# Seven half-size products for the mixer's v with u, its gates and its output, gates and branches token-major, second half of the tokens reversed

## The chip, the cores and the metric

The kernel runs on one core of one Trainium2 chip. The metric is the device time of one execution in microseconds; lower is better. Work is split over TensorE (PE; its weight loads are shown as PEld), VectorE (DVE), ScalarE (ACT), GpSimd (POOL) and SyncE (SP). SP issues most DMAs, POOL those that accumulate and some others.

## The reference

Two layers, each of three residual steps, then a last RMSNorm; 512 tokens, 1024 channels, float32:

```python
for l in range(DEPTH):
    x = x + 0.5 * swiglu(rms_norm(x, ffn1_norm[l]), ffn1_w_in[l], ffn1_w_out[l])
    x = x + mixer(rms_norm(x, mix_norm[l]), ...)
    x = x + 0.5 * swiglu(rms_norm(x, ffn2_norm[l]), ffn2_w_in[l], ffn2_w_out[l])
return rms_norm(x, final_norm)

def mixer(h, ...):
    z = h @ w_in                      # q, k, v, u: 512 columns each; ga, gf: 1024 each
    y_na = neighbourhood_attention(q, k, v, rpb) @ w_na_out
    y_f = fourier_mix(u) @ w_f_out    # real part of a 2-D DFT over tokens and 128 channels
    return (sigmoid(ga + b0) * y_na + sigmoid(gf + b1) * y_f) @ w_o
```

The feed-forward part has 2816 hidden columns.

## The kernel before

**Arithmetic.** Each float32 operand is split into a high part in the matmul's own format (ACT, L277) and a low part, the difference (DVE, L278). `mm3` (L270) makes three matmuls of each product: high x high, high x low, low x high, 512 columns each.

**Weights.** A `Stream` (L235) walks a fixed list of items, each a 128 x 1024 piece. A piece is loaded by SP up to eight items ahead; `prep` (L165) splits it into `whi` and `wlo`, two items ahead of use, in three buffers each. In the mixer a raw piece takes a slot of the pool that activations use (23 slots of 4 KB a partition); in the feed-forward stages it has nine buffers of its own, in the space where the mixer keeps its bias, mask and temporary tiles. `swap_pools` (L995) goes from one to the other, and loads of the next stage begin there.

**Feed-forward stages.** `stage_ffn` (L410) works token-major: tokens stand on the output's partitions, and activations are the operand loaded into the array. The 1024 x 1024 by 1024 x 1024 products are done with seven products of half size (Strassen's scheme): products numbered 1 to 7, taken in the order 1, 5, 6, 2, 7, 3, 4, each of 24 matmuls (`product`, L390). Products 5, 6, 7 and 4 take sums or differences of activation quarters (t1, t2, t3, t4: `combo`, L456), made once a stage behind 96 plain matmuls. Weight sums come partly from accumulating DMAs on POOL (L154), partly from DVE additions (L171). `snap` (L510) copies a partial sum from PSUM, `less` (L516) subtracts it later.

**Norm.** `Norm.quad` (L337) transposes a quarter of x to channel-major by PE and splits it. `rstd` (L362) makes the scale of each token by some 13 tiny DVE operations. For the mixer, each 256-wide piece is split straight from PSUM (L281 on DVE).

**Mixer.** `stage_mixer` (L651) runs, a layer: `proj_U` (L697) with a mirrored copy of the second half of the tokens, since the token DFT takes sums and differences of token t and its mirror; `proj_V` (L741); the token transform `four_pos` (L758) on u's sums and differences; projections of q and k channel-major, 24 matmuls each; the channel transform `four_ch` (L776); eight attention blocks in a three-deep pipeline `att_step` (L894: scores, then transposes of the softmax, then the product with v); and for each of eight groups of 128 output channels two gates of 24 matmuls, the Fourier branch and the attention branch of 12 each, channel-major, where the token scale is spread over partitions as `R` (L382). The gates' biases are one value per partition, taken by ACT's tanh. Attention steps 6 to 9 stand between the first gates and branches. Last, the output product of 192 matmuls adds into x token-major (L978).

Each engine takes its instructions in a fixed order that the build decides; a wait holds all that stands behind it on that engine. POOL and SP issue their DMAs in such an order too.

## Time and profile before

| what | value |
|---|---|
| median of 3 runs | 1978.1 us (1977.86 to 1979.02) |
| the profiled execution | 1976.79 us |
| its span | 1975.0 us |
| mean granted clock of TensorE | 0.995 |
| HBM read, written | 321.43 MB, 2.10 MB |

The span runs from the first to the last instruction of the execution; the rest of its time lies around it. A row of the profile gives a line of the code, the engine, what is written from what, the count, busy time and mean nanoseconds of one, then the idle time of that engine just before, with what ended it. Matmuls overlap, so a matmul's own duration is longer than the step from one start to the next. Rows of stretches give span, busy time and instruction count of each engine, the granted clock of TensorE, the share of the DMA engines and GB/s.

### The profile page before, as it was taken

What the parts mean: (1) busy time and instruction counts of PE and PEld (TensorE: products, weight loads), DVE (VectorE), ACT (ScalarE), POOL (GpSimd) and SP (SyncE); (2) the same over time, 40 slices, a digit from 0 to 9 for tenths busy, and PEclk for the clock granted to TensorE, in tenths of its full rate; (3) what the DMA queues carried; (4) which work ended last, traced back from release to release, by engine and by line L of the source; (5) the groups of instructions that cost most, each with busy time, mean ns of one, the idle gap of its engine ahead of it and who ended that gap; (6) DMA issues with size and microseconds to landing.
All of it is one profiled execution on the core that took longest, in us unless ns stands there. A gap on an engine that the chain in (4) does not pass through costs nothing.

```text
span 1975.0 us, 24363 instructions
## 1 busy us (share of the span) xinstructions
PE 1942.8 (98%) x9077; PEld 1608.9 (81%) x9077; DVE 1516.8 (77%) x1835; ACT 1056.6 (54%) x1520; POOL 156.6 (8%) x194
## 2 busy tenths in 40 slices
PE   8999999999999999999999999999999999999997
PEld 6888887888888888888788888878888888888885
DVE  7677899598444777889977878996874447787897
ACT  7555666445333655566555556653553336555663
POOL 0011011200000000101000100102100000000010
PEclk9999999999999999999999999999999999999998
DMA  9577599232423367749757765974123234776692
GB/s 300 162 189 202 157 246 326 75 89 65 137 75 119 86 180 195 198 147 263 226 142 205 187 171 172 283 251 113 60 80 123 96 97 105 213 176 168 178 289 103
DMA packets 96630, 328.27 MB, mean 166 GB/s; under 512 B 11136, under 2 KB 13312, under 8 KB 96512
## 3 DMA queue, kind: packets, MB, share of 16 engines
q1 hardware_dynamic: 76416, 258.55, 38.6%
q0 software_dynamic: 20096, 68.17, 19.0%
q8 instruction: 71, 1.16, 0.2%
q14 instruction: 47, 0.39, 0.1%
HBM read 321.43 MB, written 2.10 MB: 164 GB/s over the span
## 4 chain that ended last, share of the span: by engine, by line
PE 87%; DVE 9%; issue 2%; ACT 2%; DMA 1%; SPq 0%; DVEq 0%; ACTq 0%
PE A L271 7%; PE A L272 7%; PE A L273 7%; PE ps L272 7%; PE ps L271 7%; PE ps L273 7%; PE o L272 5%; PE o L273 5%; PE o L271 5%; PE B L272 4%; PE B L271 4%; PE B L273 4%; DVE wlo L278 2%; PE tr L426 2%; PE C L272 2%; PE C L273 2%
## 5 line engine op out<-in xcount | busy, mean ns | idle before, releaser
L278 DVE TENSOR_TENSOR wlo<-raw,whi 128x1024 fp32r<-128x1024 f32 (+1 forms) x498 | 597.6, 1206 | 314.8 <-ACT whi L277 313.9
L277 ACT ACTIVATE whi<-raw 128x1024 fp32r<-128x1024 f32 (+1 forms) x498 | 515.1, 1037 | 534.0 <-PE A L273 122.0
L154 POOL DMA_DIRECT2D raw<-in_wst_dram x128 | 110.5, 873 | 1515.3 <-DMA raw<-in_wst_dram 1188.5
L171 DVE TENSOR_TENSOR raw<-raw,raw 128x1024 f32<-128x1024 f32 (+1 forms) x128 | 151.1, 1190 | 2.4
L271 PE MATMUL ps<-xh,whi 128*128 128x512 f32 x384 | 151.4, 394 | 0.0
L272 PE MATMUL ps<-xl,whi 128*128 128x512 f32 x384 | 149.8, 390 | 0.0
L273 PE MATMUL ps<-xh,wlo 128*128 128x512 f32 x384 | 149.7, 390 | 0.0
L273 PE MATMUL A<-whi,xl 128*128 128x512 f32 x320 | 124.7, 390 | 0.0
L271 PE MATMUL A<-whi,xh 128*128 128x512 f32 x320 | 124.6, 389 | 0.0
L272 PE MATMUL A<-wlo,xh 128*128 128x512 f32 x320 | 124.6, 389 | 0.0
L173 ACT ACTIVATE whi<-raw 128x1024 fp32r<-128x1024 f32 x64 | 66.2, 1035 | 60.0 <-PE B L273 33.2
L271 PEld LDWEIGHTS ps<-xh,whi 128*128 128x128 f32 x384 | 72.1, 188 | 16.4
L273 PEld LDWEIGHTS ps<-xh,wlo 128*128 128x128 f32 x384 | 72.1, 188 | 15.1
L272 PEld LDWEIGHTS ps<-xl,whi 128*128 128x128 f32 x384 | 72.2, 188 | 14.4
L174 DVE SCALAR_TENSOR_TENSOR wlo<-raw,whi 128x1024 fp32r<-128x1024 f32 x64 | 75.3, 1189 | 10.8 <-ACT whi L173 10.8
L271 PEld LDWEIGHTS A<-whi,xh 128*128 128x128 f32 x320 | 60.1, 188 | 12.4
L272 PEld LDWEIGHTS A<-wlo,xh 128*128 128x128 f32 x320 | 60.1, 188 | 12.4
L273 PEld LDWEIGHTS A<-whi,xl 128*128 128x128 f32 x320 | 60.1, 188 | 12.4
L513 ACT ACTIVATE sn<-A 128x512 f32<-128x512 f32 x80 | 47.8, 599 | 41.2 <-PE A L273 41.2
L271 PE MATMUL A<-whi,t2h 128*128 128x512 f32 x160 | 63.0, 394 | 3.2 <-ACT sn L513 3.2
L271 PE MATMUL B<-whi,t1h 128*128 128x512 f32 x160 | 64.1, 402 | 1.1 <-ACT whi L277 1.1
L272 PE MATMUL B<-wlo,t1h 128*128 128x512 f32 x160 | 63.2, 395 | 0.5 <-DVE wlo L278 0.5
(257 smaller groups left out, 4804.4 us busy)
## 6 DMA issues: line engine op xcount, KB each, us to landing
raw<-in_wst_dram SPq DMA_DIRECT2D x450, 512.0 KB
raw<-in_wst_dram POOLq DMA_DIRECT2D x120, 512.0 KB, 8.1
raw<-in_wst_dram SPq DMA_DIRECT2D x32, 256.0 KB
vs<-v SPq DMA_DIRECT2D x12, 256.0 KB
bw<-in_rpb_dram SPq DMA_DIRECT2D x32, 68.0 KB
xt<-in_xtr_dram SPq DMA_DIRECT2D x8, 256.0 KB
x<-in_xin_dram SPq DMA_DIRECT2D x4, 512.0 KB
raw<-in_wst_dram POOLq DMA_DIRECT2D x8, 256.0 KB, 8.2
```

The costliest lines, as they stand in the source:

```text
L154: G.dma_start(out=self.t, in_=wst[GRAN_AT[self.plus]][:, 0 : self.n], accum_op=ALU.add)
L171: V.tensor_tensor(t, t, self.add.t, ALU.add)
L173: S.activation(hi, t, AF.Copy, scale=-1.0)
L174: V.scalar_tensor_tensor(lo, t, -1.0, hi.bitcast(F32), ALU.mult, ALU.subtract)
L271: PE.matmul(ps, lh, rh, start=start, stop=False, skip_group_check=again)
L272: PE.matmul(ps, lh, rl, start=False, stop=False, skip_group_check=again)
L273: PE.matmul(ps, ll, rh, start=False, stop=stop, skip_group_check=again)
L277: S.activation(hi, src, AF.Copy)
L278: V.tensor_tensor(lo, src, hi.bitcast(F32), ALU.subtract)
L426: PE.transpose(tr[:, k, b * P : (b + 1) * P], a[:, b, (q + k) * P : (q + k + 1) * P], ident)
L513: S.activation(t[:, b, :], ps[b], AF.Copy)
```

## The change

The mixer's three large products go over to the seven-product scheme of the feed-forward stages, with the functions `product`, `snap`, `less`, `combo` moved out so that both use them:

- v and u together are one 1024-column product; the gates are two blocks (first and second 512 columns of both gates); the output product is one. Weight pieces of a layer rise from 48 to 72 items (7 x 2 for each of four products, 8 for q and k, 4 each for the branches), with four accumulating DMAs a product.
- The norm keeps the mixer's raw quarters and splits them 1024 wide. t1, t2, t3 and t4 are made in the first product block, written to DRAM (`park`) and read back for the gates (`unpark`), all by POOL's queue.
- The second half of the tokens stands in reverse order in the mixer's activations, so that no mirrored copy is needed; q, k, y and the attention output are turned back, or written turned, in their own copies. v's second half is mirrored by four matmuls with a flipped identity. The shifted copies of v are now issued by POOL.
- Gates and branches are token-major: scale and bias enter by one DVE operation per 512 columns (the bias is spread over partitions by DMA), the Fourier branch is computed in groups of 12 matmuls beside attention steps 6 to 9 and behind them, the attention branch in `merge` after each gate block.
- The merged result is transposed to channel-major (`to_channels`, 16 transposes a half) and combined for the output's seven products; `put` adds each into x.

The diff, cut to its core (the weight layout and the functions that only moved are left out):

```diff
+            strassen(s, lambda q: "v" + q, 0, two, order)
+            for i in range(8):
+                add(Raw((s, "qk", i)))
+            for i in range(2):
+                for g in range(2):
+                    add(Raw((s, "f", i, g)))
             st += 1
+            for i in range(2):
+                strassen(s, lambda q: "g" + q, i, two, order)
+                for g in range(2):
+                    add(Raw((s, "n", i, g)))
+            strassen(s, lambda q: "w" + q, 0, two, order)
...
-                    if self.mix:
-                        split(hq[:, kt, :], lq[:, kt, :], tr[:, k, :], self.gain(4 * i + kt))
-                    else:
-                        S.activation(raw[:, kt, :], tr[:, k, :], AF.Copy, scale=self.gain(4 * i + kt))
-            if not self.mix:
-                split(hq, lq, raw)
+                    src = tr[:, k, ::-1] if self.mix and j else tr[:, k, :]
+                    S.activation(raw[:, kt, :], src, AF.Copy, scale=self.gain(4 * i + kt))
...
+        def park(m, acts):
+            t = dp.tile([2, P, 1024], F32, tag=f"park{m}", name=nm("park"))
+            for z in range(2):
+                G.dma_start(out=t[z], in_=acts[z].rearrange("p a b -> p (a b)").bitcast(F32))
+            keep[m] = t
+            return acts
+        def unpark(m):
+            res = []
+            for z in range(2):
+                a = slot(F32R, "tk")
+                G.dma_start(out=a.rearrange("p a b -> p (a b)").bitcast(F32), in_=keep[m][z])
+                res.append(a)
+            return res[0], res[1], 0
...
+        acts = {1: (hx[0], lx[0], 0), 2: (hx[1], lx[1], 0), 3: (hx[1], lx[1], 256)}
+        b11, b12 = raw[0, 0], raw[0, 1]
+        acts[5] = park(5, combo(b11, b11, b12, ALU.subtract, "t1"))
+        pa = pair("A")
+        product(pa, acts[1], K4, True)
+        s1 = snap(pa)
+        norm.settle()
+        b21, b22 = raw[1, 0], raw[1, 1]
+        pb = pair("B")
+        product(pb, acts[5], K4, True)
+        sb = snap(pb)
+        V.tensor_tensor(b12, b12, b22, ALU.subtract)
+        acts[6] = park(6, combo(b22, b22, b11, ALU.add, "t2"))
+        acts[7] = park(7, parts(b12, "t3"))
+        acts[4] = park(4, combo(b21, b21, b22, ALU.subtract, "t4"))
+        norm.rstd()
...
+        product(pa, acts[6], K4, False, again=True)
+        s2 = snap(pa)
+        pc = pair("C")
+        product(pc, acts[2], K4, True)
+        less(pc, s1)
+        for b in range(2):
+            vt.append(v_parts(s1[:, b, :], rm[:, b : b + 1]))
+        product(pa, acts[7], K4, False, again=True)
+        less(pa, sb)
...
+        product(pb, acts[3], K4, False, again=True)
+        less(pb, s2)
+        for b in range(2):
+            vm.append(v_parts(s2[:, b, :], rm[:, 2 + b : 3 + b]))
+            S.activation(sb[:, b, :], sb[:, b, :], AF.Copy, scale=rm[:, 2 + b : 3 + b])
+        product(pa, acts[4], K4, False, again=True)
+        for b in range(2):
+            both = []
+            for op in (ALU.add, ALU.subtract):
+                w = tmp(s="ue")
+                V.scalar_tensor_tensor(w, pa[b], rm[:, b : b + 1], sb[:, b, :], ALU.mult, op)
+                hi, lo = hilo("u")
+                split(hi, lo, w)
+                both.append((hi, lo))
+            u.append(both)
...
+        flip = sp.tile([P, P], F32R, tag="flip", name=nm("flip"), bufs=1)
+        S.activation(flip, mirror, AF.Copy)
+        for b in (1, 0):
+            t = slot(F32R, "v", (2, T))
+            for z in range(2):
+                ps = bank()
+                PE.matmul(ps, flip, vm[b][:, z, :], start=True, stop=True)
+                S.activation(t[:, z, :], ps, AF.Copy)
+            vt.append(t)
...
+            t = slot(F32R, "vs", (2, T))
+            G.dma_start(out=t[0:64].bitcast(F32), in_=vt[i][64:128].bitcast(F32))
+            G.dma_start(out=t[64:128].bitcast(F32), in_=vt[i + 1][0:64].bitcast(F32))
+            vs.append(t)
...
+            V.tensor_tensor(t[:, 0:256], ps[:, 0:256], R[:, 0:256], ALU.mult)
+            V.tensor_tensor(t[:, 511:255:-1], ps[:, 256:512], R[:, 256:512], ALU.mult)
...
+        def rows_of(src, tb, w):
             ps = bank()
-            dense(ps, xs)
-            t = tmp(s="g")
-            V.tensor_tensor(t, ps, R, ALU.mult)
-            col = (l * 2 + which) * DT + mt
-            S.activation(t, t, AF.Tanh, bias=gb[:, col : col + 1], scale=0.5)
-            return t
-        u = proj_U()
-        vt = proj_V()
+            t = slice(tb * P, (tb + 1) * P)
+            for kt, (h_, l_) in enumerate(src):
+                wh, wl = w[kt // 2]
+                c = slice((kt % 2) * T, (kt % 2 + 1) * T)
+                mm3(ps, h_[:, t], l_[:, t], wh[:, c], wl[:, c], kt == 0, kt == 3)
+            return ps
...
+        def fourier_rows(i, tb, w):
+            if tb % 2 == 0:
+                fs[i, tb // 2] = slot(F32, "fs", (2, T))
+            ps = rows_of(yf, tb, w)
+            S.activation(fs[i, tb // 2][:, tb % 2, :], ps, AF.Copy)
...
+        def gate_block(i, bias, acts, mid):
+            def arg(src, which, j):
+                t = src if src is not None else slot(F32, "ga", (2, T))
+                for b in range(2):
+                    c = 2 * j + b
+                    V.scalar_tensor_tensor(
+                        t[:, b, :], pa[b] if src is None else t[:, b, :], rm[:, c : c + 1],
+                        bias[which][:, i * T : (i + 1) * T], ALU.mult, ALU.add,
+                    )
+                S.activation(t, t, AF.Tanh, scale=0.5)
+                return t
+            def with_f(t, j):
+                f = fs[i, j]
+                V.scalar_tensor_tensor(f, t, 1.0, f, ALU.add, ALU.mult)
+            pa = pair("A")
+            product(pa, acts[1], K4, True)
+            s1 = snap(pa)
+            mid()
+            pb = pair("B")
+            product(pb, acts[5], K4, True)
+            sb = snap(pb)
+            product(pa, acts[6], K4, False, again=True)
+            s2 = snap(pa)
+            pc = pair("C")
+            product(pc, acts[2], K4, True)
+            less(pc, s1)
+            ga = [arg(s1, 0, 0)]
+            product(pa, acts[7], K4, False, again=True)
+            less(pa, sb)
+            with_f(arg(sb, 1, 1), 1)
+            product(pb, acts[3], K4, False, again=True)
+            less(pb, s2)
+            ga.append(arg(s2, 0, 1))
+            product(pa, acts[4], K4, False, again=True)
+            with_f(arg(None, 1, 0), 0)
+            return ga
+        def merge(i, ga, w):
+            for tb in range(TB):
+                j, b = divmod(tb, 2)
+                ps = rows_of(o, tb, w)
+                g = ga[j][:, b, :]
+                V.scalar_tensor_tensor(g, g, 1.0, ps, ALU.add, ALU.mult)
+                if b:
+                    V.tensor_tensor(ga[j], ga[j], fs[i, j], ALU.add)
+        mq = {}
...
+        def to_channels(i, ga):
+            for j in range(2):
+                mq[i, j] = slot(F32, "mq")
+                for q in range(2):
+                    tr = bank("tr").rearrange("p (a b) -> p a b", a=2)
+                    for k in range(2):
+                        for b in range(2):
+                            d = (2 * q + k) * P
+                            PE.transpose(tr[:, k, b * P : (b + 1) * P], ga[j][:, b, d : d + P], ident)
+                    S.activation(mq[i, j][:, 2 * q : 2 * q + 2, :], tr[:, :, ::-1] if j else tr, AF.Copy)
...
+        fill = fourier_fill()
+        next(fill)
+        for i in range(6, 10):
+            att_step(i)
+            next(fill, None)
+        bias = []
+        for which in range(2):
+            b_ = slot(F32, "gb", (D,))
+            src = bass.AP(tensor=gbias.tensor, offset=gbias.offset + (2 * l + which) * D, ap=[[0, P], [1, D]])
+            nc.sync.dma_start(out=b_, in_=src)
+            bias.append(b_)
+        for m in (5, 6, 7, 4):
+            acts[m] = unpark(m)
+        for _ in fill:
+            pass
         swap_pools(0)
-        for i in range(2):
-            ps = [bank("wo") for _ in range(TB)]
-            for g in range(4):
-                wh, wl = ws.next()
-                for kk in range(2):
-                    kt = 2 * g + kk
-                    mh, ml = m[kt]
-                    c = slice(kk * T, (kk + 1) * T)
-                    for tb in range(TB):
-                        t = slice(tb * P, (tb + 1) * P)
-                        mm3(ps[tb], mh[:, t], ml[:, t], wh[:, c], wl[:, c], kt == 0, kt == DT - 1)
-                if i == 1 and g == 1:
-                    for j in range(2):
-                        nxt.quad(0, j)
-            for tb in (range(TB) if i == 0 else (2, 3, 0, 1)):
-                v = x[:, tb, i * T : (i + 1) * T]
-                V.scalar_tensor_tensor(v, ps[tb], 0.5, v, ALU.mult, ALU.add)
-                if tb % 2:
-                    nxt.squares(i, tb // 2)
+        ga0 = gate_block(0, bias, acts, lambda: None)
+        merge(0, ga0, [ws.next(), ws.next()])
+        ga1 = gate_block(1, bias, acts, lambda: to_channels(0, ga0))
+        a1 = parts(mq[0, 0], "m1")
+        m00, m01 = mq[0, 0], mq[0, 1]
+        a5 = combo(m00, m00, m01, ALU.subtract, "m5")
+        merge(1, ga1, [ws.next(), ws.next()])
+        pa = pair("wA")
+        product(pa, a1, K4, True)
+        put(pa, 0, 0, -1)
+        to_channels(1, ga1)
+        pb = pair("wB")
+        product(pb, a5, K4, True)
+        put(pb, 1, 1, -1)
+        m10, m11 = mq[1, 0], mq[1, 1]
+        a3 = parts(m11, "m3")
+        V.tensor_tensor(m01, m01, m11, ALU.subtract)
+        a6 = combo(m11, m11, m00, ALU.add, "m6")
+        a2 = parts(m10, "m2")
+        a7 = parts(m01, "m7")
+        a4 = combo(m10, m10, m11, ALU.subtract, "m4")
+        product(pa, a6, K4, False, again=True)
+        put(pa, 0, 1, -1)
+        pc = pair("wC")
+        product(pc, a2, K4, True)
+        put(pc, 0, 0, 1)
+        nxt.squares(0, 0)
+        product(pa, a7, K4, False, again=True)
+        put(pa, 1, 1, 1)
+        nxt.squares(1, 1)
+        nxt.quad(0, 0)
+        product(pb, a3, K4, False, again=True)
+        put(pb, 0, 1, 1)
+        nxt.squares(0, 1)
+        product(pa, a4, K4, False, again=True, hook=lambda: nxt.quad(0, 1))
+        put(pa, 1, 0, 1)
+        nxt.squares(1, 0)
...
+    def put(ps, i, j, sign):
+        for b in range(2):
+            v = x[:, 2 * j + b, i * T : (i + 1) * T]
+            V.scalar_tensor_tensor(v, ps[b], 0.5 * sign, v, ALU.mult, ALU.add)
```

263 lines of the change are left out of this document (99 added, 164 removed).

## Prediction

> **What bounds the kernel now.** I read the page's shares first, then the slices, the chain, and busy time by stretch.
>
> ```profile
> PE 1942.8 (98%) x9077; PEld 1608.9 (81%) x9077; DVE 1516.8 (77%) x1835; ACT 1056.6 (54%) x1520; POOL 156.6 (8%) x194
> ...
> PE   8999999999999999999999999999999999999997
> ...
> DVE  7677899598444777889977878996874447787897
> ...
> PEclk9999999999999999999999999999999999999998
> ...
> PE 87%; DVE 9%; issue 2%; ACT 2%; DMA 1%; SPq 0%; DVEq 0%; ACTq 0%
> ```
>
> TensorE is the bound nearly everywhere. DVE's slices vary: 9 where a feed-forward stage ends, 4 in the second half of each mixer. The stretches of the first mixer (340 to 642 us), with the stage end before it and the run's opening, have the columns span, PE, PEld, DVE, ACT, POOL, clock, DMA share, GB/s:
>
> ```profile
> 280.00:340.00 60.00, 59.62 (x271) 49.16 (x270) 59.57 (x64) 35.63 (x45) 7.56 (x11) 1.00 0.97 318
> 340.00:360.00 20.00, 18.79 (x85) 14.67 (x84) 15.33 (x38) 11.94 (x25) 1.00 (x2) 1.00 0.44 144
> 360.00:400.00 40.00, 40.00 (x201) 33.93 (x200) 23.15 (x28) 14.47 (x18) 10.74 (x14) 1.00 0.40 106
> 400.00:500.00 100.00, 98.35 (x555) 81.29 (x554) 86.24 (x157) 53.10 (x124) 9.11 (x12) 1.00 0.23 70
> 500.00:642.00 142.00, 142.00 (x642) 118.08 (x641) 65.69 (x78) 46.56 (x61) 1.77 (x2) 1.00 0.35 111
> 510.00:600.00 90.00, 90.00 (x399) 74.56 (x398) 42.41 (x49) 29.80 (x34) 0.00 (x0) 1.00 0.31 108
> 30.00:50.00 20.00, 15.13 (x55) 11.00 (x54) 16.58 (x35) 11.09 (x18) 1.72 (x2) 0.86 0.90 226
> ```
>
> PE idles only 2.9 us in the mixer (1.2 in 340:360, 1.7 in 400:500). DVE is busy 190 of these 302 us, so 111 us are free, mostly beside gates and output. The stretch 30:50 shows what happens when DVE must make activation combinations without that cover: 4.9 us of PE lost in 20, and the clock falls.
>
> **What goes.** Each of three groups of 192 or 384 full matmuls becomes 7/8: U with V 192 to 168, gates 384 to 336, output 192 to 168, so 96 fewer a layer. Four mirror matmuls and 32 transposes come.
>
> ```profile
> 82.79 1.91 PE L426 MATMUL tr<-ident,th 128*128 128x128 f32 x16
> ...
> 84.45 0.48 PE L271 MATMUL B<-whi,t1h 128*128 128x512 f32 x1
> ```
>
> Start to start, 399 matmuls fill 90 us (0.226 each); 16 transposes take 84.45 - 82.79 = 1.66 (0.104 each). A layer saves 92 x 0.226 = 20.8, less 32 x 0.104 = 3.3: **17.5 us a layer, 35.0 in all**, if PE never waits more than before.
>
> **What comes on DVE.** Its pitches and Activation's duration:
>
> ```profile
> 319.43 3.68 DVE L537 SCALAR_TENSOR_TENSOR x<-o,x 128x512 f32<-128x512 f32 x6
> 323.02 1.22 DVE L278 TENSOR_TENSOR wlo<-raw,whi 128x1024 fp32r<-128x1024 f32 x1
> ...
> 333.81 3.49 DVE L278 TENSOR_TENSOR wlo<-raw,whi 128x1024 fp32r<-128x1024 f32 x3
> 337.22 1.22 DVE L531 TENSOR_TENSOR at<-at,at 128x1024 f32<-128x1024 f32 x1
> ...
> 353.94 0.16 DVE L367 TENSOR_TENSOR ms<-ssq 128x4 f32<-128x4 f32 x1
> 354.14 0.17 DVE L368 TENSOR_SCALAR ms<-ms 128x4 f32<-128x4 f32 x1
> ```
> ```profile
> L277 ACT ACTIVATE whi<-raw 128x1024 fp32r<-128x1024 f32 x470 | 497.8, 1061 | 520.5 <-PE A L273 122.0 <-PE o L273 92.3 <-PE C L273 56.7
> ```
>
> So 1024-wide 1.14 us, 512-wide 0.60, tiny ones 0.20; ACT 1.06 per 1024-wide copy. Per layer DVE gains 24 weight low halves, 16 weight additions, 11 operations on output combinations, 8 on first-stage combinations and 8 wide ones in gate merging (67 x 1.14 = 76), and 18 subtractions, 24 gate or merge operations and 6 residual updates (48 x 0.6 = 29). It loses 48 gate and m operations of 512 (29) and some flips and narrow splits (3). Net +73: 263 of 285 us. It still fits on average, so the places decide. I followed each engine's built instruction order with these durations.
>
> *First product block (U and V).* PE reaches the third product 48 matmuls and 8 transposes after the feed-forward end: 10.8 + 0.8 = 11.7 us. DVE then still has in front of t2's low half: two x updates (the second needs the last feed-forward matmul) and twelve 1024-wide operations (t1, t2, t3's differences, low halves, weights, a quad): 1.2 + 13.7 + 0.2 = 15.1, entering 0.3 to 1.2 late. That is 15.4 to 16.3, and PE can do two matmuls first: a wait of 3 to 4. Up to the last low half of u DVE has 28 wide, 20 of 512 and 15 tiny operations, 31.9 + 12.0 + 3.0 = 47; PE has 168 matmuls, 8 transposes, 4 mirrors, 39.7. The transform (L758) needs u at once; the old proj_V (L741) stood between and is gone. Floor with DVE never waiting: 47 - 39.7, less a microsecond of transform that can start early, = 6. My walk through the order, with DVE waiting for Activation's halves (which wait for three weight buffers), gives 5.5 more. Less the 1.2 idled there before: 5 to 12, I take **10**, as the walk is nearer to 30:50, where the same waits stand.
>
> *Attention.* Steps 6 to 9 now have 12 Fourier matmuls (2.7 us) beside them where 24 or 48 stood. Their waits so far:
>
> ```profile
> 425.94 0.63 PE L867 MATMUL ps<-ident,s 128*128 128x128 f32 x4 [0.51 <-ACT s L851]
> 454.85 0.74 PE L867 MATMUL ps<-ident,s 128*128 128x128 f32 x5 [0.70 <-DVE s L856]
> ```
>
> These are with 24 matmuls as cover. 2.7 us of cover go, and some 1.6 us of DVE work for q or k with them: about 1.2 more in each of three steps, **3.5** a layer, bounds 1 (latency hidden) and 6 (nothing hidden).
>
> *Gate start.* t1 to t4 return from DRAM (4 MB) as attention ends, on POOL's queue. Behind these eight stands the accumulation for the second half of product 5's weights. SP brings the biases (1 MB) and four half-megabyte weight pieces; with that accumulation, 7.5 MB. At the 318 GB/s of 280:340 that takes 23.6 us.
>
> ```profile
> raw<-in_wst_dram POOLq DMA_DIRECT2D x120, 512.0 KB, 8.1
> ```
>
> An accumulation lands 8.1 us after issue, with an emptier queue. From the end of attention to the need are four Fourier groups, product 1 and half of product 5, 10.8 + 5.4 + 2.7 less 2.2 for the halves = 17. Late by 6.9 if nothing starts earlier, 0 if 2 MB do, since slots come free during attention: **3**, midway. Parking itself (4 MB out in the first block) I cost at nothing: the first reader of a parked slot, s2's copy, comes over 15 us after t1 is ready. If that cover failed, it is the same 3.
>
> *Gate blocks.* 14 weight low halves, 4 additions and the gate work are about 32 us of DVE beside 38 us of PE: no wait.
>
> *Output block.* Product 6 is reached after 48 matmuls and 16 transposes, 12.5. Only then is the second bank of product 5 updated into x (2 x 0.6), and a sum, a weight half, a weight addition and product 6's low half follow (4 x 1.14): 18.3, plus 0.2 to start. Five matmuls stand ahead of that need (1.1): **5**, bounds 4.5 and 8 (43.5 us of DVE beside 41.4 of PE may stall it again).
>
> **A falling clock.** The run's opening and end show what a wait adds:
>
> ```profile
> 34.00:36.00 2.00, 0.93 (x5) 0.43 (x3) 0.17 (x2) 1.04 (x1) 0.68 (x1) 1.00 1.09 252
> 36.00:38.00 2.00, 1.40 (x4) 0.87 (x5) 1.95 (x3) 0.02 (x1) 0.18 (x1) 0.88 0.96 164
> 38.00:40.00 2.00, 2.00 (x6) 1.51 (x6) 0.95 (x3) 1.43 (x2) 0.86 (x1) 0.50 1.05 217
> 40.00:42.00 2.00, 2.00 (x8) 1.60 (x7) 2.00 (x3) 0.57 (x1) 0.00 (x0) 0.77 0.87 279
> ```
> ```profile
> 36.07 0.73 PE L271 MATMUL B<-whi,t1h 128*128 128x512 f32 x2 [1.14 <-ACT whi L277]
> 37.33 0.65 PE L272 MATMUL B<-wlo,t1h 128*128 128x512 f32 x1 [0.53 <-DVE wlo L278]
> ...
> 47.41 0.52 PE L271 MATMUL A<-whi,t2h 128*128 128x512 f32 x1 [3.20 <-ACT sn L513]
> ...
> 1957.46 0.80 PE L273 MATMUL o<-whi,c4l 128*128 128x512 f32 x1 [4.08 <-DVE c4l L278]
> ```
>
> Waits of 1.14 and 0.53 halve the grant for about 3.4 us; lost: 2 x (0.12 + 0.50 + 0.23) = 1.7 us of PE. After t2's wait the slow stretch is partly time in which PE would wait again; after u and after product 6 it is not. Two a layer: **3**, bounds 0 and 5. The Trainium skill (TensorE: Matmul & The Clock Gate, Why this matters for your kernels) says that gaps up to about 3 us do not bring the clock down. The first pair of rows speaks against it; by the rule the wait for u, split into short ones, would cost no clock, and the sum would be some 3 us lower over both layers.
>
> **Sum.** Per layer 10 + 3.5 + 3 + 5 + 3 = 24.5 of new waits against 17.5 saved: +7, over two layers +14. The profiled execution took 1976.8 (span 1975.0 and 1.8 around it), so 1990.8; the median, 1978.1, lies 1.3 above it: **1992**.
>
> **Rivals.**
> 1. *DVE runs ahead.* Where the waits stay at their floors (5 + 1 + 0 + 4.5 + 0 = 10.5), a layer saves 7 and the run ends near 1964: **faster**. Place: the combinations at both ends of the mixer. It decides at 17.5 us of waits a layer. For it: 280:340, where DVE is busy 59.57 of 60 and PE still loses only 0.4. Against: 30:50, and the built order, which puts t2's and product 6's halves behind work that ends after PE's arrival.
> 2. *DMA.* The return of t1 to t4 collides with gate weights and that accumulation waits its full 6.9 or more, with a cold clock behind it: 5 to 8 more a layer, about 2005. For: 30:50 and 280:340 show shares of 0.90 and 0.97. Against: 400:500 stands at 0.23, so early slots would be filled early.
> 3. *The busiest engine's own saving.* If relieving the busiest engine decides, all 35 come: 1943. For: PE 98%, chain 87%. Against: the 73 us a layer on DVE. Beside it stands the Trainium skill (Perfetto Trace Analysis, Identifying the Most-Contended Engine): optimize first the engine with the highest occupancy.
>
> **Numbers.** Forecast (DVE-bound ends) 0.57, its own range 1980 to 2003; DMA 0.13; waits that balance the saving 0.10; DVE ahead 0.17; full saving 0.03. All floors give 1964; all ceilings (12 + 6 + 7 + 8 + 5 = 38) give 1978.1 + 2 x 20.5 = 2019. Cutting the tails: 1966 to 2014. A difference of 0.2%, 4 us, is about what a measurement of this kernel can tell. Faster 0.20, same 0.10, slower 0.70.
>
> **What would show it.** Right: PE idle of 3 us or more before the first t2 matmul, before u's transform and before m6, released by DVE, with granted clock near 0.5 behind; DVE above 9 tenths in the first 55 us of a mixer; gates at full PE. Wrong: PE idle in the mixer under 35 us in both layers together (then faster), or the longest waits released by DMA into tk or raw (rival 2).

## The result and the profile after

The changed kernel takes **2023.35 us** (median of 4 runs, 2022.06 to 2026.97) against 1978.56 for the kernel before: 1.023 times as long, 95% interval 1.0212 to 1.0247. Slower, as forecast, but by 45 us in place of 14, and outside the range. The profiled execution took 2023.52 us, with a span of 2021.7.

The page of the changed kernel: shares of busy time, PE and granted clock in 40 slices, and the chain that ended last.

```profile
PE 1929.3 (95%) x8957; PEld 1591.9 (79%) x8957; DVE 1660.7 (82%) x1954; ACT 1148.5 (57%) x1636; POOL 214.9 (11%) x270
...
PE   7999999799899999999999999997998999999997
...
PEclk9999999899999999999999999998999999999999
...
PE 70%; DVE 16%; DMA 6%; issue 5%; ACT 2%; POOL 1%; SPq 0%; DVEq 0%; POOLq 0%; ACTq 0%
```

PE is busy only 13.5 us less (1942.8 before) while the span is 46.7 longer. PE's share of the chain fell from 87% to 70%; DVE's rose from 9% to 16%, DMA's from 1% to 6%. The two slices where PE and the clock drop (8 and 28 of 40) are the starts of the two mixers.

To see where the time went, both traces are cut at the same four matmuls of each mixer: the first main run of c4 in the feed-forward stage before, the end of the transform (`ps<-dft,u`), the first output product, the first `cl` of the next stage. Here c3 and c4 are the activations of products 3 and 4 at the end of a feed-forward stage; an h or l at the end of a name stands for the high or low part. Columns: span, then busy time of PE, PEld, DVE, ACT, POOL, granted clock, DMA share, GB/s. First layer 1 of the kernel before, then both layers of the changed one:

```profile
330.43:399.57 69.14, 67.93 (x331) 56.40 (x330) 47.41 (x75) 34.24 (x56) 14.14 (x19) 1.00 0.49 156
399.57:608.98 209.41, 207.76 (x1050) 172.34 (x1048) 140.09 (x223) 89.84 (x170) 9.11 (x12) 1.00 0.28 92
608.98:654.30 45.32, 45.32 (x210) 37.75 (x208) 20.11 (x22) 16.80 (x27) 1.77 (x2) 1.00 0.38 105
```
```profile
338.31:421.97 83.66, 69.68 (x314) 56.77 (x313) 67.50 (x76) 47.58 (x70) 27.05 (x36) 0.92 0.81 219
421.97:633.84 211.87, 199.95 (x1016) 165.34 (x1016) 166.89 (x259) 108.71 (x197) 23.25 (x32) 0.98 0.49 146
633.84:682.75 48.91, 44.92 (x202) 36.64 (x200) 42.63 (x44) 30.35 (x45) 1.72 (x2) 0.93 0.41 124
1336.45:1415.02 78.57, 67.42 (x314) 55.25 (x313) 66.22 (x77) 47.28 (x69) 29.67 (x37) 0.93 0.80 237
1415.02:1626.93 211.91, 200.13 (x1017) 165.47 (x1016) 166.90 (x259) 108.75 (x197) 23.21 (x32) 0.98 0.50 149
1626.93:1675.92 48.99, 45.00 (x202) 36.76 (x200) 42.63 (x44) 30.34 (x45) 1.72 (x2) 0.93 0.43 128
```

The three stretches are called block, middle (the rest of the transform, attention, gates) and output below. Layer 1 loses 14.5 + 2.5 + 3.6 us, layer 2 9.6 + 2.4 + 3.7 (against 69.0, 209.5 and 45.3 before). Another 10.5 lie outside the mixers: c4 starts 7.9 us later (330.43, 338.31), the feed-forward stages between the mixers lose 3.1, and the last one wins 0.5.

Span less busy time is what PE idles. In layer 1 it rises from 1.2 to 14.0 us in the block, from 1.7 to 11.9 in the middle and from 0 to 4.0 in the output; in layer 2 it becomes 11.2, 11.8 and 4.0. That is 27.0 and 24.0 us of new waits. A slow clock comes on top. In the mixer of layer 1 the grant fell to 0.50 in five stretches. In such a stretch a matmul starts 0.43 us after the one before it (at 333.20 and 333.63, beside c3) in place of 0.23, so about half of PE's busy time is lost:

```profile
373.32:380.15 6.83, 4.39 (x10) 3.51 (x11) 6.83 (x9) 2.01 (x2) 2.17 (x4) 0.50 0.85 271
386.98:390.39 3.41, 3.41 (x10) 2.24 (x9) 3.03 (x10) 0.09 (x1) 1.91 (x2) 0.50 0.45 180
414.28:417.69 3.41, 2.88 (x13) 2.88 (x14) 1.52 (x2) 2.45 (x5) 1.53 (x3) 0.50 0.56 133
537.16:543.99 6.83, 3.58 (x8) 2.65 (x9) 3.61 (x4) 2.00 (x2) 0.00 (x0) 0.50 0.87 173
649.80:656.63 6.83, 5.99 (x14) 4.41 (x15) 6.83 (x7) 2.69 (x3) 0.00 (x0) 0.50 0.21 77
```

PE is busy 20.25 us in these five, so 10.1 are lost; layer 2 has four such stretches with 16.43 us, so 8.2.

PE's longest waits in layer 1, from its timeline (start, duration, operation, and in brackets the idle time before it with what ended it):

```profile
329.60 0.73 PE L284 MATMUL o<-whi,c3h 128*128 128x512 f32 x2 [1.28 <-ACT whi L290]
331.57 0.50 PE L285 MATMUL o<-wlo,c3h 128*128 128x512 f32 x1 [1.23 <-DVE wlo L291]
...
375.76 0.80 PE L284 MATMUL A<-whi,t2h 128*128 128x512 f32 x1 [7.74 <-ACT t2h L290]
...
414.81 0.58 PE L285 MATMUL ps<-dft,u 128*128 128x256 f32 x1 [2.90 <-DMA dft<-in_dft_dram]
...
540.40 1.22 PE L284 MATMUL B<-whi,tk 128*128 128x512 f32 x2 [5.96 <-ACT whi L290]
...
650.64 0.80 PE L284 MATMUL wA<-whi,m6h 128*128 128x512 f32 x1 [3.99 <-ACT m6h L290]
```

Three of these places are the prediction's (t2h, gate start, m6h). Those at c3 and at dft are not in it. At t2h the wait was to be 3 to 4 us and is 7.7 (8.4 in layer 2). What DVE and POOL do just before it:

```profile
358.80 6.33 DVE L291 TENSOR_TENSOR wlo<-raw,whi 128x1024 fp32r<-128x1024 f32 x2
360.31 3.73 POOL L855 TENSOR_TENSOR bm<-bw,msk 128x256 f32<-128x256 f32 x5
366.58 4.68 POOL L855 TENSOR_TENSOR bm<-bw,msk 128x256 f32<-128x256 f32 x3 [2.54 <-DMA bw<-in_rpb_dram]
367.33 1.74 DVE L707 TENSOR_TENSOR xr<-xr,xr 128x1024 f32<-128x1024 f32 x1
368.99 1.72 DVE L291 TENSOR_TENSOR wlo<-raw,whi 128x1024 fp32r<-128x1024 f32 x1
372.27 1.21 DVE L291 TENSOR_TENSOR wlo<-raw,whi 128x1024 fp32r<-128x1024 f32 x1
```

Two weight halves that take 2.35 us elsewhere took 6.33, and three single ones 1.7 each, exactly while POOL adds the position bias to the mask; when POOL stops, DVE is back at 1.21. The same stood in the kernel before, unnoticed, because PE had 192 matmuls to do:

```profile
369.15 3.42 POOL L819 TENSOR_TENSOR bm<-bw,msk 128x256 f32<-128x256 f32 x5
```
```profile
370.05 3.61 DVE L278 TENSOR_TENSOR wlo<-raw,whi 128x1024 fp32r<-128x1024 f32 x1 [6.93 <-ACT whi L277]
```

The Trainium skill (SBUF — State Buffer, Who interferes with whom) says that a DVE instruction with two SBUF inputs contends with a GpSimd instruction that reads SBUF, and that the second to issue blocks until the first is done. These rows agree that DVE blocks: 3.61 us in place of 1.22 beside a run of 3.42. But the wait lasted to the end of the whole run of five additions, longer than one instruction as the rule has it. The prediction left the rule out.

### The profile page after: what moved, and what is told of

Same layout as the page of the kernel before. It is cut to its first block, busy times and chain, and to the rows that moved or that the text cites. A ratio compares the mean times of both kernels' runs of the same rounds, so it can differ in the third digit from the quotient of the medians.

```text
span 2021.7 us, 24626 instructions
## 1 busy us (share of the span) xinstructions
PE 1929.3 (95%) x8957; PEld 1591.9 (79%) x8957; DVE 1660.7 (82%) x1954; ACT 1148.5 (57%) x1636; POOL 214.9 (11%) x270
## 4 chain that ended last, share of the span: by engine, by line
PE 70%; DVE 16%; DMA 6%; issue 5%; ACT 2%; POOL 1%; SPq 0%; DVEq 0%; POOLq 0%; ACTq 0%
PE A L284 8%; PE A L285 8%; PE A L286 8%; PE B L284 4%; PE B L285 4%; PE B L286 4%; DVE wlo L291 4%; DMA raw<-in_wst_dram 4%; PE o L285 3%; PE o L286 3%; PE o L284 3%; PE C L284 2%; PE C L285 2%; PE C L286 2%; PE ps L284 2%
## 5 line engine op out<-in xcount | busy, mean ns | idle before, releaser
L290 ACT ACTIVATE whi<-raw 128x1024 fp32r<-128x1024 f32 (+1 forms) x530 | 548.9, 1038 | 528.6 <-PE A L286 144.6
L291 DVE TENSOR_TENSOR wlo<-raw,whi 128x1024 fp32r<-128x1024 f32 (+1 forms) x530 | 635.1, 1205 | 259.1 <-ACT whi L290 257.8
L174 DVE TENSOR_TENSOR raw<-raw,raw 128x1024 f32<-128x1024 f32 (+1 forms) x160 | 191.0, 1204 | 2.7
L284 PE MATMUL C<-whi,xh 128*128 128x512 f32 x208 | 81.1, 390 | 0.0
L285 PE MATMUL C<-wlo,xh 128*128 128x512 f32 x208 | 81.0, 389 | 0.0
L286 PE MATMUL C<-whi,xl 128*128 128x512 f32 x208 | 81.0, 389 | 0.0
L285 PE MATMUL B<-wlo,xh 128*128 128x512 f32 x208 | 81.0, 389 | 0.0
L286 PE MATMUL B<-whi,xl 128*128 128x512 f32 x208 | 81.0, 389 | 0.0
L284 PE MATMUL B<-whi,xh 128*128 128x512 f32 x208 | 81.0, 389 | 0.0
L285 PEld LDWEIGHTS A<-wlo,xh 128*128 128x128 f32 x368 | 69.1, 188 | 14.7 <-DVE wlo L177 0.4
L284 PEld LDWEIGHTS A<-whi,xh 128*128 128x128 f32 x368 | 69.1, 188 | 14.3
L286 PEld LDWEIGHTS A<-whi,xl 128*128 128x128 f32 x368 | 69.1, 188 | 14.3
L284 PE MATMUL A<-whi,t3h 128*128 128x512 f32 x176 | 69.8, 397 | 3.4 <-ACT sn L437 3.4
```

Of the source, the lines that this page charges most:

```text
L174: V.tensor_tensor(t, t, self.add.t, ALU.add)
L284: PE.matmul(ps, lh, rh, start=start, stop=False, skip_group_check=again)
L285: PE.matmul(ps, lh, rl, start=False, stop=False, skip_group_check=again)
L286: PE.matmul(ps, ll, rh, start=False, stop=stop, skip_group_check=again)
L290: S.activation(hi, src, AF.Copy)
L291: V.tensor_tensor(lo, src, hi.bitcast(F32), ALU.subtract)
```

## The experiments

**Theory:** the wait for t2h is DVE's chain, made late by POOL's additions; the gate-start wait is a matter of POOL's queue; m6h is missing cover. **Rivals:** the number of DVE operations alone; bytes at the gate start; DVE's whole work, so that a wait removed at one place comes back at the next. The table has all versions but e12 (us; block, middle and output as layer 1 / layer 2).

| | c4 starts | block | middle | output | median | ratio, 95% |
|---|---|---|---|---|---|---|
| before | 330.4 | 69.1 / 69.0 | 209.4 / 209.5 | 45.3 / 45.3 | 1978 | |
| changed | 338.3 | 83.7 / 78.6 | 211.9 / 211.9 | 48.9 / 49.0 | 2023.4 | 1.0212–1.0247 |
| e1 no additions | 338.5 | 72.9 / 72.9 | 211.8 / 212.4 | 47.9 / 47.6 | 2007.5 | 1.0126–1.0160 |
| e5 additions later | 335.9 | 72.6 / 71.5 | 218.9 / 221.2 | 49.0 / 48.0 | 2019.5 | 1.0194–1.0224 |
| e2 queues | 337.8 | 82.4 / 80.3 | 203.9 / 203.9 | 49.7 / 49.7 | 2008.2 | 1.0125–1.0180 |
| e3 order | 338.8 | 82.3 / 82.1 | 212.6 / 212.8 | 47.6 / 47.5 | 2024.7 | 1.0221–1.0260 |
| e6 order, bound | 337.7 | 83.7 / 82.1 | 214.1 / 212.5 | 47.7 / 47.7 | 2028.9 | 1.0242–1.0272 |
| e4 plain block | 338.3 | 72.0 / 72.9 | 217.0 / 217.6 | 49.0 / 47.8 | 2015.5 | 1.0175–1.0208 |
| e7, e10 plain output (e10) | 339.7 | 86.6 / 84.2 | 212.1 / 211.9 | 47.6 / 47.7 | 2031.0 | 1.0246–1.0277 |
| e8 all mends | 334.8 | 68.2 / 66.6 | 207.7 / 209.5 | 46.8 / 46.3 | 1988.6 | 1.0040–1.0070 |
| e9 two more | 333.0 | 68.2 / 68.1 | 210.9 / 210.6 | 45.8 / 45.7 | 1986.2 | 1.0038–1.0064 |
| e11 additions on DVE | 335.4 | 72.7 / 75.2 | 219.9 / 215.6 | 47.0 / 47.6 | 2018.2 | 1.0183–1.0213 |

### e1: without GpSimd's additions

```
                 res = mp.tile([P, 3, 256], F32, tag="bm", name=nm("bm"), bufs=4)
-                b = mp.tile([P, BIAS_F], F32, tag="bw", name=nm("bw"), bufs=2)
...
-                    G.tensor_tensor(
...
+                nc.sync.dma_start(out=res, in_=mask)
```

> The changed kernel without GpSimd's addition of the position bias to the mask (24 additions a layer and the loads of the bias go; one transfer brings the mask alone, so the attention here leaves the position bias out). Theory A: GpSimd's additions slow VectorE's wide operations beside them (two of them took 6.33 us at 358.80), and that is why the wait for t2h is 7.7 us and not the 3 to 4 of the prediction. Then VectorE keeps its 1.14 us pitch from 353 to 375, the wait for t2h falls to 3 to 4 us in both layers, and the run ends near 2013 (8 to 12 us less than 2023). Rival B: the number of operations ahead of t2l and Activation's turn set the wait, and GpSimd only happens to run then: the wait stays above 6.5 us and the run ends within 3 us of 2023.

PE's timeline at the first matmul of t2:

```profile
369.90 0.50 PE L284 MATMUL A<-whi,t2h 128*128 128x512 f32 x1 [2.65 <-ACT t2h L290]
```

The wait falls from 7.74 to 2.65 us (8.42 to 2.66 in layer 2), the block by 10.8 and 5.7. The run is 16 us shorter, more than the 8 to 12 expected. That is as theory A has it.

### e5: the additions later, and the opening's order

```
-            G.dma_start(out=t[64:128].bitcast(F32), in_=vt[i + 1][0:64].bitcast(F32))
+            moved = G.dma_start(out=t[64:128].bitcast(F32), in_=vt[i + 1][0:64].bitcast(F32))
...
+                    with tc.issue_after(moved.ins):
                         G.tensor_tensor(
...
+    V.tensor_single_scalar(gb, gb, 0.5, ALU.mult)
```

> The changed kernel with two edits at places far apart. (1) All of GpSimd's position-bias additions are queued behind the last of the six transfers that make vs, so they run beside the transform and no longer beside the first product block; nothing is left out. (2) The gate biases are again loaded once and halved on VectorE at the start, as in the kernel before, though nothing reads them. Theory A for (1): VectorE and GpSimd block each other; the stretch from c4's start to the transform's end falls from 83.7 and 78.6 us to about 73 to 75, as without the additions (72.9), and a little comes back in the transform or the attention: 12 us less in all. Rival B: it was the loads of the bias, or the fewer transfers, that helped there: the stretch stays above 78. Theory A for (2): the feed-forward stage at the opening ran 3.5 us later only because the missing operation let the build put VectorE's work in another order: c4 then starts 3 to 4 us earlier, near 335. Rival B: c4 starts at 338 again. Together: near 2007 by both theories A, near 2020 by both rivals.

With the whole computation in place the block falls as without the additions (72.6, 71.5). But the middle rises by 7.0 and 9.3, so only 4 us are left of the gain of both edits, and the run ends near where the rivals had it. POOL's and DVE's timelines of this kernel, beside the transform:

```profile
408.48 4.07 POOL L857 TENSOR_TENSOR bm<-bw,msk 128x256 f32<-128x256 f32 x6
...
416.63 6.79 POOL L857 TENSOR_TENSOR bm<-bw,msk 128x256 f32<-128x256 f32 x6 [4.09 <-DMA bw<-in_rpb_dram]
```
```profile
408.52 4.31 DVE L805 TENSOR_TENSOR bt<-m,m 128x256 f32<-128x256 f32 x1
...
414.40 0.43 DVE L805 TENSOR_TENSOR bt<-m,m 128x256 f32<-128x256 f32 x1
...
418.20 2.93 DVE L292 TENSOR_TENSOR b<-bt,b 128x512 fp32r<-128x512 f32 x3
421.05 0.68 DVE L804 TENSOR_TENSOR m<-ps,rot 128x512 f32<-128x512 f32 x1
```

An operation of 0.43 us took 4.31: it came 0.04 us after POOL's six additions had begun and stood until all six were done. In the second run the engines take turns (three operations in 2.93, POOL's six in 6.79). The one with an operand in PSUM (`ps`) took its usual 0.68 in the middle of that run. So the mechanism is shown; moving the additions moves its price.

The second edit acts on the very first stage: PE's longest wait there is 6.32 us in the changed kernel and 3.64 here. Loading and halving gate biases that nothing reads brings the old instruction order of the opening back, and c4 starts 2.5 us sooner (3 to 4 expected). The diff had dropped that one tiny DVE operation; the build then ordered DVE's work otherwise.

### e2: the two queues

```
-                G.dma_start(out=a.rearrange("p a b -> p (a b)").bitcast(F32), in_=keep[m][z])
+                nc.sync.dma_start(out=a.rearrange("p a b -> p (a b)").bitcast(F32), in_=keep[m][z])
...
+                G.dma_start(out=dfs[c][hl], in_=dft[hl, c])
...
         acts[5] = park(5, combo(b11, b11, b12, ALU.subtract, "t1"))
...
-                G.dma_start(out=dfs[c][hl], in_=dft[hl, c])
```

> The changed kernel with the four loads of the transform's constants put ahead of the parks on GpSimd's queue, and with the return of t1 to t4 put on SyncE's queue. Theory A: both waits are a matter of the queue: the 2.90 us wait for dft in layer 1 goes, and the accumulation of product 5's second weight piece no longer stands behind eight returns, so the wait at the gates' start falls from 5.96 and 5.80 us to under 3: 9 to 11 us less, near 2013. Rival B: at the gates' start the bytes are the limit (the DMA engines are busy over 0.95 there), so that wait stays above 5 us or moves to the biases or weights, and only the 3 us of dft go: near 2020.

The middle in layer 1, then the place where a wait came back:

```profile
420.22:624.09 203.87, 197.92 (x1016) 164.32 (x1016) 167.02 (x259) 108.89 (x197) 18.99 (x24) 1.00 0.52 155
```
```profile
389.94 0.59 PE L384 MATMUL ps<-r,ident 128*128 128x2 f32 x2 [2.77 <-DVE r L307]
```

The gate-start wait is gone in both layers and the middle 8.0 us shorter, 6 of wait and 2 of slow clock, with the same bytes: the queue, not the bandwidth. The Trainium skill (DMA: Bandwidth & Descriptors, Issuing engine by pattern) gives simple loads and stores to Sync; this run agrees, by 8 us a layer. The dft wait went too, but the block won 1.3 us only: DVE was as late as before, and the mirror matmul of r now waits 2.77. In layer 2, which had no dft wait, the block took 1.7 us more.

### e3 and e6: product 2 ahead of product 6

In both the weights of `"v"` and `"w"` come in that order; the diff is e6's, and e3 lacks the `with` line:

```
-        product(pa, acts[6], K4, False, again=True)
-        s2 = snap(pa)
         pc = pair("C")
-        product(pc, acts[2], K4, True)
+        two = product(pc, acts[2], K4, True)
+        with tc.issue_after(two.ins):
+            product(pa, acts[6], K4, False, again=True)
+        s2 = snap(pa)
```

> The changed kernel with the products of the first and of the output block in the order 1, 5, 2, 6, 7, 3, 4 in place of 1, 5, 6, 2, 7, 3, 4: product 2 needs no combination and gives VectorE 24 matmuls (5.4 us) more before t2 and m6 are read. Theory A: the waits are a matter of cover at one place: the wait for t2h falls from 7.7 and 8.4 us to 2 to 3, that for m6h from 4.0 to 0, and with them the slow clock behind: 20 us less in all, near 2003. Rival B: VectorE's whole work in the block is the bound, and what is saved at t2h comes back at t3, at t4 or at u: the first block ends no more than 2 us earlier, only the output block gains 4 to 5 a layer, and the run ends near 2012.

> The order 1, 5, 2, 6, 7, 3, 4 again, this time with product 6 bound behind product 2 on TensorE's queue (in the first try the build put product 6 ahead again, in part). Theory A: cover decides: the wait for t2h (7.7, 8.4) falls to 2 to 3, the stretch from c4's start to the transform's end falls by 4 to 6 us in both layers, the output block by 2 to 4: near 2007. Rival B: VectorE's whole work in the block is the bound, so that the time comes back as waits at products 6, 7, 3 or 4: the stretch falls by less than 2 us, and the run ends near 2020.

Neither came out as theory A had it in the first block, and both runs ended later than either theory had them. PE there, in e3 and in e6:

```profile
378.40 0.80 PE L285 MATMUL A<-wlo,t2h 128*128 128x512 f32 x1 [4.55 <-DVE wlo L291]
```
```profile
382.67 0.58 PE L384 MATMUL ps<-r,ident 128*128 128x2 f32 x2 [15.30 <-DVE r L307]
```

In e3 the build put part of product 6 ahead again, now with its weights prepared after product 2's. In e6 product 6 stood right, but the mirror matmul of r stood ahead of product 2 and waited 15.3 us for DVE. Both are inconclusive for the block: the sum of DVE's work or the place of r would do as well. In the output block both give 1.2 to 1.5 us, less than theory A's 4 to 5 (e3) and 2 to 4 (e6).

### e8: all mends together

Both edits of e5, both of e2, the bound order of e6, and `norm.rstd(); norm.spread(R)` moved behind product 2.

> All mends together: gate biases loaded as before, GpSimd's additions behind vs, the transform's constants early, t1 to t4 returned on SyncE's queue, both orders 1, 5, 2, 6, 7, 3, 4 bound, and the chain of r moved behind product 2. If the parts add up (gate start 8 a layer, additions 6 to 8 a layer, opening 3.5, dft 3, order 5 to 8 a layer): 2023 less 44 to 54, so 1970 to 1980, about the time of the kernel before. Theory that VectorE's whole work in the block is the bound: the order gives nothing and the run ends at 1988 to 1995.

```profile
334.77:402.95 68.18, 65.73 (x314) 54.58 (x313) 59.39 (x77) 47.77 (x70) 15.87 (x28) 0.97 0.82 253
402.95:610.66 207.71, 200.61 (x1017) 165.94 (x1016) 169.91 (x258) 109.06 (x197) 25.85 (x33) 0.99 0.52 154
```
```profile
371.93 0.50 PE L285 MATMUL A<-whi,t2h 128*128 128x512 f32 x1 [0.27 <-ACT whi L291]
```

With product 2 ahead and r behind it the waits in product 6 are 0.27 and 0.57, and the block is 4.4 to 4.9 us shorter than in e5: cover does decide once r doesn't stand ahead of it (the two were changed together, so their shares are not known). The time, 1988.6, is in the range of the second theory, though the order did give something, against that theory. 35 us of the loss are mended; still 0.55% slower than before (0.40 to 0.70). The three stretches of a mixer now sum to 322.7 and 322.4 us, against 323.9 and 323.8 before: the mixers themselves are a little faster. What stays of the loss lies in the feed-forward stages, some 13 us: c4 starts 4.4 later, 657.2 from `cl` to the next c4 against 650.6, and 2.2 in the last stage.

### e4 and e10: parts undone

e4 makes v and u by 192 plain matmuls, and t1 to t4 behind them. e10 makes the output plainly (e7 was the same with the two off-diagonal quarters added to each other's quarter of x: 2028.3, expected as e10).

Of e10's diff the core; e4 does the same to `"v"`:

```
-            strassen(s, lambda q: "w" + q, 0, two, order)
+            for q in "abcd":
+                for g in range(2):
+                    add(Raw((s, "w" + q, 0, g)))
...
-        product(pa, a1, K4, True)
...
+                                mm3(ps[j][b], lh, ll, wh[:, k, :], wl[:, k, :], n == 0, n == DT - 1)
```

> The changed kernel with v and u made by eight plain half-size products again (192 matmuls in place of 168, u first; second half of the tokens still reversed), and t1 to t4 made behind them for the gates. Theory A: the first product block is where the change lost most (from the last feed-forward products to the transform's end 17 to 23 us a layer over what its 24 fewer matmuls would give): with it undone that stretch goes back to about that of the kernel before, plus 2 us, and the run ends at 2023 - 2 x 11 to 15 = 1993 to 2001. Rival B: the loss belongs to the work that stays (combinations t1 to t4, parks, GpSimd's additions), which now falls on the transform and the attention: the run ends at 2015 or above.

> The changed kernel with the output product made plainly again (192 matmuls in place of 168; m is still turned by 32 transposes). Undoes the third part alone. Theory A (the product's own combinations make its end wait, 4.0 us at m6 with a slow clock behind): the output block, 48.9 us now, takes 46 to 49 us, as 5.4 us of matmuls come back and 5 to 7 of waits go; the run ends within 4 us of 2023. Rival B: the seven products pay here and the wait would stay with the plain product too (m's parts and the transposes cause it): 53 us or more a layer, near 2032.

> The changed kernel with the output product made plainly (192 matmuls in place of 168; m still turned by 32 transposes), with each quarter of the product added to its own quarter of x. Theory A (the combinations make the output block's wait, 4.0 us at m6 with a slow clock behind): the block, 48.9 us now, takes 46 to 49 us, as 5.4 us of matmuls come back and 5 to 7 of waits go; the run ends within 4 us of 2023. Rival B: m's parts and the transposes make the wait with the plain product too: 53 us or more a layer, near 2032.

e4's block and middle, then e10's output:

```profile
338.31:410.33 72.02, 70.75 (x343) 58.47 (x342) 47.36 (x60) 35.83 (x55) 25.28 (x25) 1.00 0.44 139
410.33:627.35 217.02, 203.16 (x1013) 167.24 (x1012) 169.05 (x258) 112.39 (x201) 28.26 (x41) 0.97 0.55 164
```
```profile
638.45:686.08 47.63, 47.63 (x226) 39.45 (x224) 23.18 (x23) 19.92 (x32) 1.75 (x2) 1.00 0.41 122
```

e4's block keeps PE nearly full at clock 1.00 and wins 11.7 and 5.7 us, as theory A had it; but the middle, where the combinations now stand beside the transform, takes 5 to 6 more, and the run, 8 us shorter, ends where rival B had it. In the changed kernel seven products lose to eight in the output as well: 47.6 plain against 48.9. With the mended order they win: 46.8 and 46.3 in e8, though the output of the kernel before, which has no transposes, takes 45.3. And e8's first block (68.2, 66.6) is shorter than e4's (72.0, 72.9) and than that of the kernel before. e10's total of 2031 is no measure of the output product: its block was 3 to 6 us longer, with dft waits of 2.21 and 3.31 in layer 1.

### e9, e11, e12: more covers, another engine

e9 and e11 start from e8, e12 from the kernel before. First e9's two edits, then that of e11 and e12:

```
-        next(fill)
         for i in range(6, 10):
             att_step(i)
-            next(fill, None)
+            for _ in range(2):
+                next(fill, None)
...
+        two = product(pb, a3, K4, False, again=True)
+        put(pb, 0, 1, 1)
```
```
-                        G.tensor_tensor(
+                        V.tensor_tensor(
```

> The kernel with all mends, and two more. (1) In the last attention steps two Fourier groups (24 matmuls, 5.4 us) stand behind each step in place of one, and none is left behind the attention. (2) The output products go 1, 5, 2, 3, 6, 7, 4, so that product 3, which needs no combination, also stands ahead of m6. Theory A (cover at one place decides): the waits of 1.74, 1.26 and 1.31 us in the last steps go (4.3 a layer), and the wait for m6h (1.69 us and 1.8 of slow clock) goes (3 a layer): 1988.6 less 14, near 1974, a little under the kernel before. Rival B: with the Fourier groups moved up, t1's return and the gate weights are due 8 us sooner and are late at the gates' start (3 to 6 us a layer): 1980 to 1988, no better than before.

> The kernel with all mends, with the 24 additions of bias and mask a layer made by VectorE in place of GpSimd. Theory A (the two engines block each other, and a run of six additions holds VectorE for 4 to 5 us, more than the six cost on VectorE itself, about 6 x 0.42): the first attention waits (0.98, 1.41) and the slow transform shrink, 2 to 4 us a layer: 1981 to 1985. Rival B: 24 x 0.42 = 10 us more on VectorE a layer, in a stretch that it bounds, cost as much as the blocking did: 1987 to 1994.

> The kernel before, with the same 24 additions a layer made by VectorE in place of GpSimd. Theory A (there TensorE covers what the blocking costs; it idles only 2.9 us in the first mixer): within 3 us of 1978, either way. Rival B: the blocking cost something in the kernel before too, or the additions load VectorE where it is late: over 4 us away from 1978.

In e9 product 3 comes before product 6, but both take their weights from one running sum. So product 3's weights lack a term that the sum gets only at product 6, and product 6's hold one too many: the work is the same, the output is not the reference's. It gained nothing that can be told from e8. The time is within rival B's range, but the cause it named is not what shows: the waits moved, to 3.07 us at the step whose own Fourier group had gone, to 1.20 at the gates, and in the output to 1.55 and 1.51 at m6l and m7h. e11 missed on both theories:

```profile
395.96 0.43 DVE L859 TENSOR_TENSOR bm<-bw,msk 128x256 f32<-128x256 f32 x1 [4.83 <-DMA bw<-in_rpb_dram]
```
```profile
398.90 1.65 PE L768 MATMUL ps<-v,flip 128*128 128x512 f32 x3 [5.57 <-DVE v L295]
```

An addition takes 0.43 us, but DVE stood 4.83 us at one whose bias hadn't landed, with v's halves queued behind it. In e8 POOL stood 5.51 us at such a load and PE did not wait for it. The middle's 12.2 and 6.1 us over e8 are only in part explained: PE idles 11.4 us there in layer 1 against 7.1, at a granted clock of 0.95 against 0.99. e12 in the kernel before: 1982.9, ratio 1.0016 to 1.0035, 5.3 us more, so rival B by a little. No version tried beats the kernel before.

## Why the prediction was wrong

Per layer the prediction's own terms come, by stretch, to +7.0 for the block (10 + 1.5 for the clock, less 20 matmuls x 0.226), -2.7 for the middle (3.5 + 3 + 1.7 for transposes, less 48 x 0.226) and +2.7 for the output (5 + 1.5 + 1.7, less 24 x 0.226). Measured: +14.5 and +9.6, +2.5 and +2.4, +3.6 and +3.7, and 10.5 outside the mixers. By kind: the new waits are 27.0 and 24.0 us against the 21.5 of the forecast, the slow clock took 10.1 and 8.2 against 3, and the feed-forward stages 10.5 against nothing. Of the 31 us by which the forecast was low, the waits make 8, the clock 12 and the feed-forward stages 10.5.

- **The saving** of matmuls was right: with the gate-start wait mended, the middle takes 203.9, and 209.4 - 10.8 + 1.7 + 3.5 = 203.8.
- **The clock, 3 a layer with bounds 0 and 5: mis-sized**, the step inside the mixers that failed most. That waits bring a slow clock was right. But "two a layer" at 1.7 us of loss each came from one short slow stretch of the opening, and the trace of before had a longer one: 0.50 from 1955.81 to 1962.64, around the wait of 4.08 us that the prediction shows. The changed kernel has five slow stretches in layer 1 and four in layer 2, of 3.41 or 6.83 us, with 10.1 and 8.2 us lost.
- **First block, 10: the right size by luck.** The new waits there are 12.8 and 9.9 us. But "my walk through the order" used undisturbed durations, and without POOL's collision (e5) they are only 4.2, below its floor of 5:

```profile
335.85:408.48 72.63, 67.23 (x314) 55.42 (x313) 60.16 (x76) 47.79 (x70) 14.06 (x25) 0.95 0.80 235
```

  The walk's extra waits for Activation did not show in PE's time, and the collision it left out did. The collision costs 11 us of the block in layer 1 and 7 in layer 2, slow clock included, the former with the dft wait. Such a row stood in the trace of before (DVE 3.61 us for one weight half) and wasn't read, because PE didn't wait there.
- **Place of the wait: half right.** It stands at t2h, as forecast, but the wait "before u's transform" is only 0.78: by then PE was late itself.
- **Parking at nothing: not shown to be wrong.** The parks stand ahead of the dft loads in e1 and e5 as well, and there dft is in time. What wasn't costed is the new place of these loads. The kernel before issues them ahead of r's way through DRAM; the changed one behind it, where POOL's queue stood 11.41 us for the row to land (before, then changed):

```profile
338.14 2.15 POOL L668 DMA_DIRECT2D dft<-in_dft_dram  x4
```
```profile
403.32 0.54 POOL L398 DMA_DIRECT2D R<-row  x1 [11.41 <-DMA row<-rm]
403.85 2.16 POOL L740 DMA_DIRECT2D dft<-in_dft_dram  x4
```

  In layer 1 dft came 2.90 us late; moved ahead (e2) it no longer does, but of that the block won only 1.3.
- **Gate start, 3: mis-sized.** It costs 8 (e2): 6.0 of wait and 2 of the clock. "0 if 2 MB do" start earlier counted bytes; what counted was the accumulation's place behind eight returns.
- **Attention, 3.5: about right.** Idle time in the middle, gate start aside, rose from 1.7 to 6.0 (the longest: 1.21, 0.59, 1.53, 1.25, 1.32), so 4.3 within the bounds of 1 and 6; e9 shows that these waits can be moved but not removed by that cover.
- **Output, 5: about right** as a wait, 3.99. The clock behind it was not: 0.50 over 6.83 us, 3.0 lost and not 1.5. The block came out 0.9 over the sum.
- **Outside the mixer: put at nothing, without a reason**, and 10.5 us. Part is the opening's order (2.5, e5). Another is the pair of waits at c3: it comes before both mixers now, 2.5 us of wait in layer 1 with 1.7 of slow clock behind it (332.36 to 335.77), and 3.1 in layer 2. It isn't new; the kernel before has it where the next norm keeps raw copies:

```profile
965.65 0.73 PE L271 MATMUL o<-whi,c3h 128*128 128x512 f32 x2 [1.35 <-ACT whi L277]
967.62 0.51 PE L272 MATMUL o<-wlo,c3h 128*128 128x512 f32 x1 [1.24 <-DVE wlo L278]
```

The change gives the mixer's norm such copies too (`Norm.quad`). That this is the cause is argued, not shown: no version took them away alone.

- **The rivals.** DMA (2005) was right about the place and wrong about the means: a queue, not bytes. The full saving and DVE running ahead fell with 27.0 and 24.0 us of new waits against 17.5 saved.

## What to carry to other kernels

Where DVE is going to be the bound, read the trace of before for DVE operations that are longer than their kind, and look at what POOL does at that moment; a cost that PE's cover hides is due as soon as the cover is sold. On an in-order queue ask of each transfer what stands ahead of it and for what that waits, before counting bytes. Cost a slow clock for every long wait that you forecast, not for a chosen two. Half-size products pay where their combinations lie beside other matmuls: here the gates won at once; the two ends lost as first built. With product 2, r and the additions in another order (e8) the first block came out under the kernel before, and the output under its plain form.

## What the runs showed of the hardware

POOL's additions hold a DVE operation with both inputs in SBUF for the rest of their run (0.43 became 4.31 us), or take turns with it (1.22 became 1.72 at 368.99), and leave one with an input in PSUM alone (0.68). And the clock: nearly the same pair of waits at c3 left it at 1.00 in the kernel before and at 0.87 over 26 us in e8.

```profile
957.00:983.00 26.00, 23.42 (x111) 18.93 (x110) 23.89 (x27) 17.09 (x30) 0.12 (x1) 1.00 0.69 220
```
```profile
960.00:986.00 26.00, 23.48 (x98) 18.78 (x97) 22.22 (x25) 14.38 (x25) 0.00 (x0) 0.87 0.61 191
```

What decides it these runs don't tell; in the changed kernel itself the pair left it at 1.00 at 994 us (983 to 1009) and was followed by 0.50 at 332. Single waits of 1.2 us in attention (449 us) cost no clock; around that of 3.99 at m6h it was 0.50 for 6.83 us.
